# State-space layer: gate product on ScalarE and GpSimd, a new order of the last tiles, other buffers for the next stage's inputs

## The chip, the cores and the metric

The kernel runs on one core of a Trainium2 chip. The core has a matrix engine (TensorE, PE in the profile, with PEld for its weight loads), a vector engine (VectorE, DVE), an engine for functions of one operand (ScalarE, ACT), a general engine (GpSimd, POOL) and a queue that issues the DMAs (SyncE, SP). The metric is the device time of one execution in microseconds, the median over runs; less is better.

## The reference

Two layers of a causal decoder trunk, for a sequence of 1024 tokens of width 1024, in float32:

```python
for i in range(DEPTH):                      # DEPTH = 2
    h = rms_norm(x, pre_norm)
    h = dilated_attention_mixer(h, ...) if i % 2 == 0 else s5_mixer(h, ...)
    x = x + rms_norm(h, post_norm)

def s5_mixer(h, ...):
    proj = h @ w_in                         # 1024 x 2048
    u, z = proj[..., :SSM_WIDTH], proj[..., SSM_WIDTH:]
    y = s5_scan(u, ...)                     # 64 groups of 16 channels, 64 complex states each
    g = gelu(y)
    y = g * sigmoid(g @ w_glu + b_glu)      # the GLU
    return (y * silu(z)) @ w_out
```

The change lies in the second layer, `s5_mixer`: in the product z * sigmoid(z) of its gate, in the order of the last tiles of `h @ w_in`, and in the buffers through which g reaches the GLU's matmuls.

## The kernel before, in words

**Precision by halves.** Every operand of a large matmul is held as two parts, a rounded high part and a low part that is the rest (`split`, L79 to L87: ACT makes the high part, DVE subtracts for the low part). A product is the sum of three matmuls: high by high, high by low, low by high (`proj_part`, L102). A weight tile of 128 output columns is loaded and split by `load_w` (L90); raw, high and low tiles have two buffers each, so a weight tile takes the buffers of the one two before it.

**Tiles and halves.** The tokens are two halves (th = 0, 1) of 512. A tile of a projection is one weight tile times one half: 8 blocks of depth by 3 matmuls, 24 matmuls into one bank of matmul memory (PSUM). `in_order` (L759) runs over the weight tiles and calls `use(e, th, ps)` on each result, and then `after(t)` with the running number t of the tile.

**The state-space layer** (`layer1`, L1402) has 16 weight tiles: e = 0 to 7 give u, e = 8 to 15 give z. With `start="half"` the first two weight tiles are run by token halves, all others tile by tile, both halves of one before the next. `use_u` copies u out to memory. `use_z` makes the gate, in two instructions: ACT takes tanh(z/2) into a slot, and DVE forms (tanh + 1) * z, with z read from the bank; the result is written to memory (`z_dr`).

Between the tiles runs the scan, for eight groups of channels, each in stages that `run(t)` starts at a fixed tile: loads, `ssm_input`, `ssm_taps`, `ssm_states` and `ssm_outputs`. `ssm_states` (L1347) is a chain through the engines: PE pv (L1359), three DVE products (L1360 to L1362), a GpSimd sum (L1363), four DVE scans (L1366), a GpSimd product (L1368), DVE products and X (L1370 to L1372). `ssm_outputs` (L1376) multiplies X and the taps on PE (py, L1386 and L1387), and forms the GELU: ACT (L1388, L1389), two GpSimd instructions (L1390, L1391), ACT (L1392), DVE (L1393); the result goes to memory (`y_dr`, L1394). The last group's outputs come after tile 29 of 0 to 31.

**The GLU** (`glu`, L1445) reads y back in another order (`y_view`): 16 loads of 128 x 512, 8 groups for each token half, each followed by a split into the tiles g0 and g1. Its first two weight tiles are run as a block (`start="block"`): four banks are filled over the first 7 of 8 depth blocks, in the order (0,0), (1,0), (0,1), (1,1) of weight tile and half, and then the last depth block of all four. The later weight tiles run one by one.

**Buffers.** Short-lived tiles of 128 x 512 come from a ring, `c.slot` (L50), which takes turns between two tags with 3 and 4 buffers. The pool pb has six large tiles, b0 to b5: b1 holds the taps of groups 0 to 3, b3 those of groups 4 to 7; b4 and b5 hold the high and low part of the layer's normed input for the first token half, b0 and b2 for the second. The GLU's inputs take b1 (high) and b3 (low) for the first half, b4 and b5 for the second; its weights for the output projection later take b1 and b4. The tag O (4 buffers of 128 x 1024) holds the outputs of attention, and later the two post-norm weights; in the state-space layer it is otherwise unused.

**Order of the work.** Each engine, and the SP queue, works in the order of its own list. The lists are written by a planner which simulates the program with estimated times and lets the instruction of the highest rank go that is ready by them; the rank is the place in the program, and `high_priority(AHEAD)` moves a block 600 places forward. So a change of one instruction's engine or place can shift others in all lists. An instruction that waits holds up everything behind it on its engine.

Of the kernel before, what the change touches and what calls it, by code (L numbers as in the profile page):

```python
# [15 lines left out]
F32 = mybir.dt.float32  # L16
F32R = mybir.dt.float32r
I32 = mybir.dt.int32
AF = mybir.ActivationFunctionType
ALU = mybir.AluOpType  # L20
# [3 lines left out]
P = 128  # L24
S = 1024
D = 1024
KT = 8
H = 512
# [85 lines left out]
def proj_half(c, w, h):  # L114

    pool, tag = ((c.psj, "psj"), (c.pst, "pst"))[c.banks % 2]
    c.banks += c.wide
    ps = pool.tile([P, H], F32, tag=tag, name="psj")
    proj_part(c, ps, w, h, range(KT))
    return ps  # L120
# [638 lines left out]
def in_order(c, srcs, h, use, after=None, start=None, ws=()):  # L759

    t = 0

    def one(e, th, ps):
        nonlocal t
        use(e, th, ps)
        if after:
            after(t)
        t += 1  # L770

    ws = list(ws) or [load_w(c, srcs[e]) for e in range(2 if start else 0)]
    if start == "block":
        jobs = [(e, th) + ((c.psj, "psj"), (c.psl, "psl"))[th] for th in range(2) for e in range(2)]
        pss = [pool.tile([P, H], F32, tag=tag, name="psb") for _, _, pool, tag in jobs]
        for ks in (range(KT - 1), (KT - 1,)):
            for ps, (e, th, _, _) in zip(pss, jobs):
                proj_part(c, ps, ws[e], h[th], ks)
                if ks[0]:
                    one(e, th, ps)  # L780
    elif start == "half":
        for e in range(2):
            one(e, 0, proj_half(c, ws[e], h[0]))
        pss = [c.psj.tile([P, H], F32, tag="psj", name="psj") for _ in range(2)]
        for part in range(2):
            cs = slice(part * 256, part * 256 + 256)
            for e in range(2):
                proj_part(c, pss[e][:, cs], ws[e], [x[:, :, cs] for x in h[1]], range(KT), part == 0)
                if part:
                    one(e, 1, pss[e])  # L790
    c.wide = 1 if start == "half" else c.wide
    for e in range(len(ws), len(srcs)):
        w = load_w(c, srcs[e])
        for th in range(2):
            one(e, th, proj_half(c, w, h[th]))
    c.banks = c.wide = 0

# [599 lines left out]
def y_view(c, et, th):  # L1397

    return bass.AP(c.y_dr.tensor, c.y_dr.offset + et * P * S + th * 4 * 16384, [[P, P], [16384, 4], [1, P]])


def layer1(c, a, h1, ws):  # L1402

    nc, tc = c.nc, c.tc
    c.ssm = c.es_pa.enter_context(tc.tile_pool(name="ssm", bufs=1, side="left", reuse_waits="tile"))
    def use_u(et, th, ps):
        ut = c.slot("ut")
        with tc.high_priority(AHEAD):
            nc.scalar.copy(ut.rearrange("p (i n) -> p i n", i=4)[:, ::-1, :], ps.rearrange("p (i n) -> p i n", i=4))
            dst = bass.AP(c.u_dr.tensor, c.u_dr.offset + et * P * S + (1 - th) * 4 * 16384, [[P, P], [16384, 4], [1, P]])  # L1410
            nc.sync.dma_start(dst, ut.rearrange("p (i n) -> p i n", i=4))

    def use_z(et, th, ps):
        z = c.slot("z1")
        with tc.high_priority(AHEAD):
            nc.scalar.activation(z, ps, AF.Tanh, scale=0.5)
            nc.vector.scalar_tensor_tensor(z, z, 1.0, ps, op0=ALU.add, op1=ALU.mult)
            nc.sync.dma_start(c.z_dr[et, :, th * H:th * H + H], z)

    groups = [Ssm(c, a, e) for e in range(8)]  # L1420
    c.taps = []
    at = [[] for _ in range(40)]
    for e in range(8):
        t = (11 * e + 2) // 4
        for stage, d in ((ssm_loads, (-1, 2)[e] if e < 2 else 3), (ssm_input, 5), (ssm_taps, 6), (ssm_states, 7), (ssm_outputs, 10)):
            at[t + d + 1].append((stage, e))

    def run(t):
        for stage, e in at[t + 1]:
            if stage is ssm_loads and e == 1:  # L1430
                with tc.issue_after(groups[0].load_U.ins):
                    stage(groups[e])
            else:
                stage(groups[e])

    def use(e, th, ps):
        (use_u if e < 8 else use_z)(e % 8, th, ps)

    run(-1)
    in_order(c, [a["ssm_w_in"][e] for e in range(16)], h1, use, run, start="half", ws=ws)  # L1440
    for t in range(32, 39):
        run(t)


def glu(c, a):  # L1445
    nc, tc = c.nc, c.tc
# [1 line left out]
    nc.sync.dma_start(bh, a["b_glu"])  # L1448
    nc.vector.tensor_scalar(bh, bh, 0.5, None, op0=ALU.mult)
    g, y2 = [], []  # L1450
    for th, tags in enumerate((("b1", "b3"), ("b4", "b5"))):
        g.append([c.pb.tile([P, KT, H], F32R, tag=t, name=f"g{th}{t}") for t in tags])
        for et in range(8):
            y = c.slot("gy")
            nc.sync.dma_start(y.rearrange("p (i n) -> p i n", i=4), y_view(c, et, th))
            split(c, g[th][0][:, et, :], g[th][1][:, et, :], y)
    y2.append([c.pb.tile([P, KT, H], F32R, tag=t, name=f"y0{t}") for t in ("b0", "b2")])
# [185 lines left out]
```

## Time and profile before

| what | value |
|---|---|
| median of 3 runs | 1691.89 us (1691.3 to 1694.68) |
| the profiled execution, its own time | 1692.35 us |
| its span on the core | 1690.6 us |
| mean granted clock of TensorE | 0.991 |
| PE, DVE, ACT, POOL busy | 98%, 60%, 42%, 27% of the span |
| z tiles in the state-space layer | 1375.6 to 1497.5 us |
| loads of gy, first and last issue | 1489.7, 1512.3 us |

Times in the text are microseconds from the start of the span, of that one execution. A row of a list of stretches gives its bounds and length, and then how long each engine was busy in it. A row of the chain of waits gives a start, a length, and the engine and line or the transfer that the end of the program hung on. "PE busy" counts a matmul until its modelled end, and the matmuls overlap: the pace is read from the starts or from how many ran in a stretch.

### The profile page before, as it was taken

How to read it: one execution, taken by the hardware profiler on the slowest of the kernel's cores; microseconds unless marked ns; L12 is line 12 of the kernel's file. 1: busy time of each engine (PE TensorE's matmuls, PEld its weight loads, DVE VectorE, ACT ScalarE, POOL GpSimd, SP SyncE). 2: the span in 40 equal slices, each digit the busy share in tenths (PEclk: the TensorE clock that was granted, in tenths of full speed). 3: DMA queues.
4: the chain of work that ended last, by engine and by line, in shares of the span. 5: the costliest groups of instructions: out<-in, count | busy, mean ns of one | idle time of the engine just before them, and what ended most of it. 6: DMA issues, size and time to landing. Idle time of an engine off the chain costs nothing.

```text
span 1690.6 us, 26330 instructions
## 1 busy us (share of the span) xinstructions
PE 1655.9 (98%) x9714; PEld 1395.1 (83%) x9714; DVE 1012.3 (60%) x2511; ACT 712.8 (42%) x1730; POOL 452.8 (27%) x301
## 2 busy tenths in 40 slices
PE   8999999999999999999999999998999999999998
PEld 6889999978888888888888888886888887867886
DVE  8698898625454554545455454567462788845533
ACT  5232232226456464646556464654352222243411
POOL 2000000132241514324252523303220344513121
PEclk9999999999999999999999999998999999989999
DMA  6222455531232423233142323228146978365432
GB/s 238 83 55 101 148 176 163 166 105 54 89 104 65 118 69 98 83 93 92 58 136 71 110 83 101 87 69 225 63 155 195 262 223 250 112 206 164 147 119 87
DMA packets 176857, 212.19 MB, mean 126 GB/s; under 512 B 37443, under 2 KB 133462, under 8 KB 176728
## 3 DMA queue, kind: packets, MB, share of 16 engines
q1 hardware_dynamic: 176728, 210.52, 41.7%
q8 instruction: 76, 1.25, 0.3%
q14 instruction: 53, 0.43, 0.1%
HBM read 153.51 MB, written 56.96 MB: 124 GB/s over the span
## 4 chain that ended last, share of the span: by engine, by line
PE 85%; DVE 7%; DMA 4%; issue 1%; POOL 1%; ACT 1%; SPq 0%; DVEq 0%; POOLq 0%; ACTq 0%
PE psj L110 45%; PE psq L373 10%; PE psl L471 5%; PE pso L548 4%; PE pt L499 4%; PE pso L865 3%; PE pso L866 3%; PE pso L867 3%; PE psb L110 1%; PE pso L574 1%; DVE T L1366 1%; DMA fz<-on_dr 1%; PE psv L234 1%; PE psv L233 1%; PE psv L232 1%
## 5 line engine op out<-in xcount | busy, mean ns | idle before, releaser
L110 PE MATMUL psj<-hh,whi 128*128 128x512 f32 x896 | 358.1, 400 | 0.0
L110 PE MATMUL psj<-hh,wlo 128*128 128x512 f32 x896 | 358.1, 400 | 0.0
L110 PE MATMUL psj<-hl,whi 128*128 128x512 f32 x896 | 355.2, 396 | 0.0
L84 POOL TENSOR_TENSOR wlo<-wraw,whi 128x1024 fp32r<-128x1024 f32 x48 | 115.2, 2400 | 394.8 <-ACT whi L83 379.7
L110 PEld LDWEIGHTS psj<-hh,whi 128*128 128x128 f32 x896 | 168.8, 188 | 37.0
L110 PEld LDWEIGHTS psj<-hh,wlo 128*128 128x128 f32 x896 | 168.8, 188 | 36.4
L110 PEld LDWEIGHTS psj<-hl,whi 128*128 128x128 f32 x896 | 168.7, 188 | 36.3
L488 ACT ACTIVATE lg<-lg,nm 128x128 f32<-128x128 f32 (+1 forms) x384 | 168.2, 442 | 37.0 <-DVE nm L483 37.0
L477 DVE CUSTOM_DVE_ANT_0 lg<-psl,T 128x128 f32<-128x128 f32 (+1 forms) x384 | 110.6, 347 | 89.1 <-PE psl L471 89.1
L83 ACT CAST whi<-wraw 128x1024 fp32r<-128x1024 f32 x80 | 83.7, 1046 | 161.9 <-PE psj L110 108.0
L373 PE MATMUL psq<-whi,v 128*128 128x256 f32 x640 | 120.3, 284 | 0.0
L110 PE MATMUL psj<-h1h,whi 128*128 128x512 f32 (+1 forms) x272 | 104.9, 386 | 1.1 <-ACT h1h L83 1.1
L84 DVE TENSOR_TENSOR ph<-pt,ph 128x512 fp32r<-128x512 f32 (+2 forms) x160 | 96.7, 622 | 15.3 <-ACT ph L83 13.1
L84 DVE TENSOR_TENSOR kl<-psj,kh 128x512 fp32r<-128x512 f32 x48 | 33.2, 691 | 119.3 <-ACT kh L83 118.8
L110 PE MATMUL psj<-h1l,whi 128*128 128x512 f32 (+1 forms) x272 | 104.2, 383 | 0.2 <-DVE h1l L84 0.2
L110 PE MATMUL psj<-h1h,wlo 128*128 128x512 f32 (+1 forms) x272 | 104.0, 383 | 0.0
L83 ACT CAST ph<-pt 128x512 fp32r<-128x512 f32 (+2 forms) x160 | 81.5, 529 | 46.5 <-PE pt L499 45.5
L373 PEld LDWEIGHTS psq<-whi,v 128*128 128x128 f32 x640 | 100.0, 189 | 1.2 <-issue 1.2
L373 PE MATMUL psq<-wlo,v 128*128 128x256 f32 x320 | 91.2, 285 | 0.7 <-DVE wlo L84 0.7
L548 PE MATMUL pso<-ph,vs 128*128 128x256 f32 (+1 forms) x544 | 86.6, 284 | 0.0
L499 PE MATMUL pt<-identr,lg 128*128 128x128 f32 x560 | 82.2, 276 | 0.0
L1232 POOL TENSOR_TENSOR Ks<-Ks,O 128x16 f32<-128x16 f32 x8 | 4.3, 536 | 284.5 <-ACT Ks L1230 284.5
(284 smaller groups left out, 3691.0 us busy)
## 6 DMA issues: line engine op xcount, KB each, us to landing
wraw<-in_w_in_dram SPq DMA_DIRECT2D x56, 512.0 KB
mw<-wt_dr SPq DMA_DIRECT2D x48, 256.0 KB
v<-in_w_v_dram SPq DMA_DIRECT2D x20, 512.0 KB
vp<-v_dr SPq DMA_DIRECT2D x16, 512.0 KB
wraw<-in_ssm_w_in_dram SPq DMA_DIRECT2D x16, 512.0 KB
v_dr<-v SPq DMA_DIRECT2D x30, 256.0 KB
rot_dr<-rt SPq DMA_DIRECT2D x48, 128.0 KB
ca_dr<-ca SPq DMA_DIRECT2D x32, 144.0 KB
```

The source lines that it names most:

```text
L83: nc.scalar.copy(hi, src)
L84: return (engine or nc.vector).tensor_tensor(lo, src, f32(hi), op=ALU.subtract)
L110: nc.tensor.matmul(ps, a[:, s], b[:, k, :], start=first and k == 0 and n == 0, stop=k == KT - 1 and n == 2, skip_group_check=True)
L373: nc.tensor.matmul(o, r[x][:, k, ts], w[y][:, k, :], skip_group_check=True, start=i in (0, 4, 5) and t % 2 == k == n == 0, stop=k == 3 and ...
L471: nc.tensor.matmul(psl[:, h, o], x[HEADS[h], qs], y[HEADS[h], ks], start=j == js[0] and n == 0, stop=n == 2, skip_group_check=True)
L477: nc.vector.tensor_tensor_reduce(lg[:, h, j, 0:w], psl[:, h, o], bt[:, h, 256 - w:256], scale=1.0, scalar=-3.0e38, op0=ALU.add, op1=ALU.ma ...
L488: nc.scalar.activation(lg[:, h, j, 0:w], lg[:, h, j, 0:w], AF.Exp, bias=nm[:, h, b:b + 1], accum_out=ms[:, col:col + 1])
L499: c.nc.tensor.transpose(pt[:, n * P:(n + 1) * P], lg[:, h, j, part * P:part * P + P], c.ident)
L548: nc.tensor.matmul(o, l, r, start=n == 0, stop=n == len(jobs) - 1, skip_group_check=True)
L865: nc.tensor.matmul(ps, gh[:, k, ts], wh[:, k, :], start=k == 0, stop=False)
L866: nc.tensor.matmul(ps, gh[:, k, ts], wl[:, k, :], start=False, stop=False)
L867: nc.tensor.matmul(ps, gl[:, k, ts], wh[:, k, :], start=False, stop=k == KT - 1)
```

## The change

Three edits in one:

- `use_z` takes two slots instead of one. ACT writes tanh(z/2) into the first and copies z from the bank into the second; GpSimd adds 1 to the first and multiplies the second by it. The two GpSimd instructions and the write to memory stand outside the high-priority block.
- In `in_order` with `start="half"`, the last two weight tiles are loaded together and run by token halves: (14,0), (15,0), (14,1), (15,1) instead of (14,0), (14,1), (15,0), (15,1). For the other callers `pairs` is 0 and nothing changes.
- In `glu`, y is loaded into a ring of six halves of three O tiles instead of slots, and the tiles of the GLU's inputs change: b1 and b4 for the first token half, b5 and b3 for the second.

```diff
@@ in_order
-    c.wide = 1 if start == "half" else c.wide
-    for e in range(len(ws), len(srcs)):
+    c.wide = int(start == "half")
+    pairs = 2 if start == "half" else 0
+    for e in range(len(ws), len(srcs) - pairs):
         w = load_w(c, srcs[e])
         for th in range(2):
+            one(e, th, proj_half(c, w, h[th]))
+
+    ws = [(e, load_w(c, srcs[e])) for e in range(len(srcs) - pairs, len(srcs))]
+    for th in range(2):
+        for e, w in ws:
             one(e, th, proj_half(c, w, h[th]))
     c.banks = c.wide = 0
@@ layer1
     def use_z(et, th, ps):
-        z = c.slot("z1")
+        t, z = c.slot("zt"), c.slot("z1")
         with tc.high_priority(AHEAD):
-            nc.scalar.activation(z, ps, AF.Tanh, scale=0.5)
-            nc.vector.scalar_tensor_tensor(z, z, 1.0, ps, op0=ALU.add, op1=ALU.mult)
-            nc.sync.dma_start(c.z_dr[et, :, th * H:th * H + H], z)
+            nc.scalar.activation(t, ps, AF.Tanh, scale=0.5)
+            nc.scalar.copy(z, ps)
+        nc.gpsimd.tensor_scalar(t, t, 1.0, None, op0=ALU.add)
+        nc.gpsimd.tensor_tensor(z, z, t, op=ALU.mult)
+        nc.sync.dma_start(c.z_dr[et, :, th * H:th * H + H], z)
@@ glu
-    for th, tags in enumerate((("b1", "b3"), ("b4", "b5"))):
+    ring = [x[:, n * H:n * H + H] for x in (c.outs.tile([P, D], F32, tag="O", name="gy", bufs=4) for _ in range(3)) for n in range(2)]
+    for th, tags in enumerate((("b1", "b4"), ("b5", "b3"))):
         g.append([c.pb.tile([P, KT, H], F32R, tag=t, name=f"g{th}{t}") for t in tags])
         for et in range(8):
-            y = c.slot("gy")
+            y = ring[(8 * th + et) % 6]
             nc.sync.dma_start(y.rearrange("p (i n) -> p i n", i=4), y_view(c, et, th))
             split(c, g[th][0][:, et, :], g[th][1][:, et, :], y)
```

## The prediction

> **What bounds the kernel now.** I read the stretches between the state-space layer and the output tiles first, engine by engine:
>
> ```profile
> 1477.40:1493.80 16.40, 15.25 (x81) 12.50 (x80) 7.49 (x10) 6.98 (x12) 5.12 (x5) 1.00 0.58 191
> 1493.80:1502.45 8.65, 5.17 (x10) 2.41 (x11) 6.65 (x9) 5.73 (x9) 0.00 (x0) 0.67 0.85 244
> 1502.45:1506.30 3.85, 3.85 (x11) 2.98 (x10) 1.39 (x2) 0.87 (x3) 0.00 (x0) 0.50 1.09 348
> 1506.30:1525.00 18.70, 18.55 (x78) 14.59 (x76) 8.60 (x11) 7.74 (x13) 2.91 (x3) 0.98 0.54 156
> 1525.00:1527.10 2.10, 1.20 (x5) 0.68 (x5) 2.08 (x2) 2.10 (x3) 1.31 (x2) 1.00 0.72 223
> 1527.10:1682.00 154.90, 154.90 (x667) 125.48 (x668) 67.10 (x134) 40.59 (x76) 36.19 (x27) 1.00 0.41 131
> ```
>
> Columns: stretch, length, busy time of PE, weight load, DVE, ACT, POOL, then granted clock, DMA share and rate. After 1527.10 PE is never idle at clock 1.00, so no edit there can save anything (the tags of the GLU inputs also free two buffers for the last weights earlier; that is worth nothing under this cover). The loss is at 1493.80 to 1527.10, where the state-space layer hands over to the GLU: PE is busy 5.17 of 8.65 us, and then runs 3.85 us at clock 0.50.
>
> The end of the chain of waits says on what it hangs:
>
> ```profile
> 1480.00 2.05 DMA y_dr<-Y
> 1486.11 1.77 POOL Y L1391
> 1490.13 3.85 DMA gy<-y_dr
> 1496.33 4.41 DMA gy<-y_dr
> 1501.43 22.48 PE psb L110 x84
> 1525.02 2.03 DVE wlo L84
> 1527.10 49.93 PE psj L110 x212
> 1577.49 16.86 PE psj L110 x72
> ```
>
> Undisturbed, 72 matmuls take 16.86 us, 0.2342 us each. The GLU's first block holds 4 tiles of 24, so 96, and 4 more matmuls of the next weight tile ran before 1527.10. That is 100 x 0.2342 = 23.42 us of work in 33.30 us: **9.88 us are lost here**. The cause in the chain is the load of gy, the layer's outputs read back from memory. The DMA queue in order of time:
>
> ```profile
> 1486.74 2.87 SPq L1394 DMA_DIRECT2D y_dr<-Y  x2
> 1489.67 1.59 SPq L1455 DMA_DIRECT2D gy<-y_dr  x3
> 1491.30 0.50 SPq L1418 DMA_DIRECT2D z_dr<-z  x1
> 1494.52 3.64 SPq L1455 DMA_DIRECT2D gy<-y_dr  x6
> ```
>
> No gy leaves before 1489.67, after the last group's write, although by the chain the seventh of eight groups was written from 1480.00. The loads use slots of the two-tag ring that the z tiles hold too, and the low halves of the first GLU half go into b3, which holds the taps of groups 4 to 7.
>
> Two smaller waits lie inside the layer:
>
> ```profile
> PE py L1387 <- DVE X L1372: 2.1, 1, 2.1
> ...
> PE py L1387 <- POOL Y L1391: 1.1, 1, 1.1
> ```
>
> ```profile
> 1414.90:1418.40 3.50, 3.47 (x16) 3.48 (x17) 2.90 (x4) 0.08 (x1) 0.05 (x1) 0.51 0.94 321
> ```
>
> The 2.1 us wait is followed by 3.50 us at clock 0.51, which did 16 matmuls; half of the stretch, about 1.7 us, is lost to the clock. So the layer loses 2.1 + 1.7 + 1.1 = 4.9 us.
>
> The Trainium skill (TensorE: Matmul & The Clock Gate, Part 1: The HAM clock gate) says that the clock falls to half after an idle window of about 3.4 us. The half agrees with 0.50 and 0.51, the length does not: one 2.1 us wait was enough here. By the page's rule a leftover wait of 2 us would cost 2 us; by the trace it costs nearly 4, and I go by the trace.
>
> **The inputs' ring and the tags.** Nothing is added: still 16 loads, 16 casts and 16 subtractions. Three O tiles give six halves, and nobody else writes them after the attention output stage. So the first six loads wait only for their group's outputs, and can leave before 1480. The low halves now go into b4, the high half of the layer's first normed input, which is free when the tiles of the first token half are done; by the new tile order that is two tiles before the layer's end, 2 x 24 x 0.2342 = 11.2 us ahead of 1493.8, instead of one tile. What is late next: group 6 and 7's loads, then the eight of the other half, which need the ring halves back. In the queue above, three loads took 1.59 us and six took 3.64 us to issue, and the chain gives 3.85 and 4.41 us for a load with its wait; ten loads from about 1482 are in by about 1500, and the second token half starts 21 matmuls x 2 tiles = 9.8 us after 1493.8, at 1503.6. So the waits on gy should go, and the slow clock with them. Bounds: the whole 9.88 us, or nothing if the loads do not move.
>
> I leave 1.0 us in the block, for one late operand; the wait for the next GLU weights stays, since their buffer is freed only in the block's last matmuls. Before, 1525.00 to 1527.10 was 2.10 us for 4 matmuls' 0.94, 1.2 us lost; I take 1.3. Saved: 9.88 - 1.0 - 1.3 = **7.6 us**.
>
> **The last tiles by token halves.** The same 96 matmuls, reordered. Weights 15 are now needed one tile earlier, and their buffer is that of weights 13:
>
> ```profile
> 1462.60 1.05 ACT L83 CAST whi<-wraw 128x1024 fp32r<-128x1024 f32 x1 [6.57 <-PE psj L110]
> ...
> 1479.28 1.03 ACT L83 CAST whi<-wraw 128x1024 fp32r<-128x1024 f32 x1
> ```
>
> ```profile
> 1471.79 1.19 DVE L84 TENSOR_TENSOR wlo<-wraw,whi 128x1024 fp32r<-128x1024 f32 x1
> ```
>
> ```profile
> 1465.98 0.39 PE L1387 MATMUL py<-X,CA 128*128 128x128 f32 x2
> ```
>
> Tile (14, first half) starts when group 6's py matmuls end at about 1466.2 and takes 24 x 0.2342 = 5.6 us, to 1471.8. The third matmul of (15, first half) wants the low part at about 1472.3; where DVE has it now it ends at 1472.98. I take 0.7 us, between 0 (DVE reaches it earlier, having lost two z products before it) and 2.5 (a wait of 1.2 and the clock). The weight buffer of the GLU's tile 0 is freed one tile later too, at about 1488 where its cast now runs at 1479.28. Cast and subtraction take 1.03 + 1.19 = 2.2 us, done by 1491, before 1493.8: nothing, with 2.8 us of cover.
>
> **The gate halves.** The DVE product leaves, an ACT copy and two GpSimd instructions come, 16 times, from 1375 to 1494. The groups of that time (line, busy, mean ns, idle):
>
> ```profile
> L1391 POOL TENSOR_TENSOR Y<-Y,Y 128x512 f32<-128x512 f32 x12 | 17.5, 1460 | 0.8
> ...
> L1371 DVE TENSOR_TENSOR T<-Sg,T 64x512 f32<-64x512 f32 x10 | 13.8, 1377 | 0.2
> ...
> L1417 DVE SCALAR_TENSOR_TENSOR z<-z,psj 128x512 f32<-128x512 f32 x16 | 10.8, 677 | 0.7 <-ACT z L1416 0.7
> ...
> L1416 ACT ACTIVATE z<-psj 128x512 f32<-128x512 f32 x16 | 9.3, 591 | 21.1 <-PE psj L110 21.1
> ...
> L1390 POOL TENSOR_SCALAR Y<-Y 128x512 f32<-128x512 f32 x12 | 8.6, 720 | 12.9 <-ACT Y L1389 12.2
> ...
> L1361 DVE TENSOR_TENSOR T<-Sg,pv 64x512 f32<-64x512 f32 x9 | 6.2, 690 | 0.1
> ```
>
> ```profile
> 1375.00:1493.80 118.80, 115.54 (x619) 98.27 (x617) 96.61 (x131) 36.05 (x59) 56.59 (x54) 0.99 0.62 185
> ```
>
> ACT: 16 x 0.591 = 9.5 us more on 36.05 of 118.80, hidden under its idle time; a matmul bank is then free after ACT alone and no longer waits for DVE. POOL: 16 x (0.720 + 1.460) = 34.9 us more on 56.59, so 91.5 of 118.8. These are in order with the scan's own steps (L1363, L1368) and the GELU's (L1390, L1391): a pair ahead of one of them makes it 2.2 us late, then DVE's X and PE's py behind it. The z writes on the SP queue now wait for POOL as well, and the loads behind them wait with them. DVE: 16 x 0.677 = 10.8 us less. But L1371 takes 1377 ns where L1361, of the same shape, takes 690: the one that reads two operands from SBUF is stretched by 0.69 us on average beside POOL's work. If each pair stretches one such instruction, 16 x 0.69 = 11.0 us come back, and DVE stays at 96.8.
>
> The Trainium skill (SBUF — State Buffer, Who interferes with whom) speaks against this edit: a DVE instruction with two SBUF inputs and a GpSimd instruction that reads SBUF lock each other out entirely. The product taken away read one operand from PSUM and, by that rule, locked nothing. If every GpSimd pair kept DVE waiting for its whole length, DVE would come to 96.6 - 10.8 + 34.9 = 120.7 us, more than the stage.
>
> So the layer's price is 0 in my sum: X comes 0.7 us earlier without a product before it, or about as much later with a stretched instruction. Bounds: 4.9 us won (both waits gone) to 15.6 us lost (first rival).
>
> **Sum.** 7.6 - 0.7 - 0 = 6.9 us. The profiled execution took 1692.35 us (span 1690.6, 1.75 around it): 1685.4. It was 0.46 above the median of 1691.89, so the runs' median becomes **1685.0**.
>
> **Rivals.**
> First, slower: GpSimd becomes the link that sets py. If in each of the last four groups, whose chains run beside z tiles, one pair stands ahead of a chain step and py has no slack, PE waits 2.2 us and loses 1.7 us to the clock: 4 x 3.9 = 15.6, 1700.6. For it: two of these groups wait already, and 81% of DVE's stage is full. Against: the other groups do not wait, and POOL is idle for half of the stage. It undoes the gain from 1.7 us a group. Chance 0.15.
>
> Second, the wait changes its owner: weights of GLU tiles 0 and 1 come after 1493.8, each 2.2 us of cast and subtraction, and 4 us of slow clock cost 2: 6.4 of the 6.9 are gone, 1691.4. For it: the two reordered tiles hold both weight buffers longer. Against: the cover of 2.8 us. Chance 0.12.
>
> Third, the change does not do what it says: the planner leaves the loads behind the last group's writes, as at 1489.67, and the block loses its 9.88 us as before: about 1692. For it: nothing but the order of one queue decides. Chance 0.06.
>
> Fourth, more: the layer's own 4.9 us go too, since a z product stood on DVE before X: 1680.1. Against: POOL's added work. Chance 0.17.
>
> **How the numbers follow.** The forecast keeps 0.50. Differences under 0.2%, 3.4 us, can't be told from none here. Faster: forecast and fourth, 0.67. Same: second (but for its lower edge) and third, 0.17. Slower: the first, and 0.01 of the second: 0.16. The forecast's own range is 1682 to 1688.5. To hold 8 in 10 I go from 1680, the fourth's time, to 1692.5, the third's, and leave out most of the first.
>
> **What would show it.** Right: gy loads leave before 1480, psb follows psj with under 1 us of waits, the clock stays near 1.00 through the block, and from the block's first matmul to the tile after it pass about 25 us instead of 33. The gate: DVE's L1371 or X stretched, POOL near 90 us in the stage. Wrong: PE's waits on py grow or appear in more groups, with clock near 0.5 behind them; or psb waits on weights; or gy still leaves after the last y_dr.

## The result: slower

The changed kernel takes 1701.03 us (median of 4 runs, 1699.99 to 1702.91), the kernel before took 1692.29 us (4 runs, 1691.3 to 1694.68). The ratio on record is **1.0055, 95% interval 1.0041 to 1.0069**; it is not the plain quotient of the two medians, which is 1.0052. The forecast was 1685.0 us, range 1680.0 to 1692.5: wrong in sign. The profiled execution of the changed kernel took 1700.58 us, its span is 1698.8 us against 1690.6, so 8.2 us longer.

Line numbers grow by 6 in the changed kernel, and by 9 behind the gate: py is L1392/L1393, X is L1378, the GELU L1394 to L1399, y_dr L1400, gy L1464. The gate is L1422 and L1423 (ACT), L1424 and L1425 (GpSimd), L1426 (write). I cut both traces at the same work: the pv matmuls of groups 4, 5 and 7, the block's first matmul, and the tile behind the block. Before, in the columns of the list of stretches:

```profile
1393.80:1420.14 26.34, 24.23 (x124) 20.74 (x123) 19.69 (x27) 8.10 (x13) 11.01 (x11) 0.94 0.94 261
1420.14:1455.30 35.16, 35.16 (x186) 29.66 (x185) 29.97 (x44) 10.07 (x16) 19.17 (x18) 1.00 0.65 193
1455.30:1493.82 38.52, 37.35 (x201) 31.36 (x199) 29.00 (x39) 11.93 (x20) 15.66 (x15) 1.00 0.38 123
1493.82:1527.10 33.28, 28.77 (x101) 20.66 (x101) 18.70 (x24) 16.44 (x25) 4.22 (x4) 0.85 0.70 205
```

After, the same stretches, then the whole layer from 1375.00, the two stretches of slow clock around the ends of its longest waits, and the rest of the program up to where the forecast's last row ended:

```profile
1393.50:1426.10 32.60, 24.06 (x123) 20.57 (x122) 20.09 (x24) 10.95 (x20) 20.86 (x17) 0.90 0.84 232
1426.10:1462.00 35.90, 35.52 (x187) 29.83 (x186) 26.00 (x32) 10.85 (x20) 30.23 (x26) 1.00 0.71 222
1462.00:1510.63 48.63, 40.26 (x201) 33.15 (x199) 46.85 (x54) 18.68 (x34) 36.89 (x28) 0.93 0.36 114
1510.63:1535.30 24.67, 24.21 (x100) 18.59 (x100) 6.52 (x8) 8.20 (x14) 9.66 (x6) 1.00 0.54 169
...
1375.00:1510.60 135.60, 118.35 (x618) 99.81 (x616) 111.00 (x128) 47.95 (x85) 104.26 (x82) 0.95 0.58 178
1417.52:1424.36 6.84, 3.34 (x15) 3.34 (x16) 6.68 (x8) 2.44 (x5) 4.98 (x3) 0.50 0.72 228
1485.80:1492.63 6.83, 5.17 (x12) 4.11 (x13) 6.68 (x7) 0.63 (x1) 6.04 (x5) 0.50 0.39 115
...
1535.30:1690.20 154.90, 154.87 (x667) 125.47 (x668) 71.05 (x137) 42.26 (x79) 38.64 (x28) 1.00 0.43 136
```

The last row is as long as before (154.90 us, 667 matmuls, clock 1.00), so everything happens ahead of it. The block of the GLU went from 33.28 to 24.67 us at clock 1.00: **8.6 us won, where the forecast said 7.6**. But the block starts 16.8 us later (1510.63 against 1493.82). Group 4 is 6.3 us longer, groups 5 and 6 0.7, the last stretch of the layer 10.1, and the first mark lies 0.3 earlier; 16.8 - 8.6 = 8.2, the difference of the spans.

PE's waits in the changed kernel from 1260 on (engine, what it waited for, us in total, times, the longest):

```profile
PE py L1393 <- DVE X L1378: 11.4, 4, 8.5
PE psj L110 <- DVE wlo L84: 5.3, 1, 5.3
...
PE psb L110 <- ACT whi L83: 0.6, 1, 0.6
```

The waits of psb on gy are gone. In their place stand one wait of 8.5 us for X in group 4, one of 5.3 us for the low part of weights 15, and around the end of each a stretch of 6.8 us at clock 0.50. Part of it passes while PE still waits: PE works at half clock for 3.3 us behind the first wait, which ends at 1421.02, and for 5.2 us behind the second, which ends at 1487.46. About half of these times is lost, 1.7 and 2.4 us.

**How group 4 became late.** GpSimd's list of the changed kernel, in order of time, with idle time and its releaser in brackets:

```profile
1377.98 1.61 POOL L1424 TENSOR_SCALAR zt<-zt 128x512 f32<-128x512 f32 x1
1379.56 1.60 POOL L1374 TENSOR_TENSOR X<-Cg,T 128x508 f32<-128x508 f32 x1
...
1381.16 1.69 POOL L1425 TENSOR_TENSOR z<-z,zt 128x512 f32<-128x512 f32 x1
...
1387.45 3.29 POOL L1397 TENSOR_TENSOR Y<-Y,Y 128x512 f32<-128x512 f32 x2
```

The gate's pair stands ahead of the GELU product of group 2 (L1397), whose two instructions end at 1390.74; before, the later of them ended at 1389.26. The planner works with estimates of such times. In the list that it wrote, both writes of that group's outputs now stand behind a run of loads in the SP queue:

```profile
1394.07 1.73 SPq L1343 DMA_DIRECT2D taps<-k_dr  x4
...
1396.37 1.35 SPq L1400 DMA_DIRECT2D y_dr<-Y  x2
```

Before, they stood on either side of three loads of taps:

```profile
1390.76 0.37 SPq L1394 DMA_DIRECT2D y_dr<-Y  x1
1391.76 1.78 SPq L1337 DMA_DIRECT2D taps<-k_dr  x3
1394.54 0.34 SPq L1394 DMA_DIRECT2D y_dr<-Y  x1
```

The next group's GELU overwrites the tile that is being written out, so ACT is held at its first step. After:

```profile
1402.39 0.60 ACT L1394 ACTIVATE Y<-py 128x512 f32<-128x512 f32 x1 [10.03 <-DMA y_dr<-Y]
```

Before:

```profile
1396.18 0.60 ACT L1388 ACTIVATE Y<-py 128x512 f32<-128x512 f32 x1 [4.34 <-DMA y_dr<-Y]
```

ACT goes on 6.2 us later. The end of that GELU (L1399) stands in DVE's list ahead of group 4's scans, so DVE waits for it, then the scans and X come, and PE behind X:

```profile
1408.13 0.69 DVE L1399 SCALAR_TENSOR_TENSOR Y<-Y,Y 128x512 f32<-128x512 f32 x1 [9.38 <-ACT Y L1398]
1410.01 3.50 DVE L1372 TENSOR_TENSOR_SCAN T<-rho,T 128x128 f32<-128x128 f32 x4 [1.18 <-POOL T L1369]
...
1419.23 1.74 DVE L1378 TENSOR_TENSOR X<-X,T 128x508 f32<-128x508 f32 x1
```

**What the pairs themselves cost.** Groups of like instructions of the changed kernel, GpSimd and DVE, 1375 to 1511 (busy time, mean ns of one, idle time before them):

```profile
L1424 POOL TENSOR_SCALAR zt<-zt 128x512 f32<-128x512 f32 x14 | 25.2, 1800 | 3.8 <-ACT zt L1422 3.8
L1425 POOL TENSOR_TENSOR z<-z,zt 128x512 f32<-128x512 f32 x14 | 20.8, 1485 | 0.7
...
L1372 DVE TENSOR_TENSOR_SCAN T<-rho,T 128x128 f32<-128x128 f32 x40 | 25.4, 694 | 3.9 <-POOL T L1369 3.6
L1377 DVE TENSOR_TENSOR T<-Sg,T 64x512 f32<-64x512 f32 x10 | 13.7, 1370 | 0.2
L1378 DVE TENSOR_TENSOR X<-X,T 128x508 f32<-128x508 f32 x10 | 12.3, 1245 | 0.5
L1376 DVE TENSOR_TENSOR T<-Sg,T 64x512 f32<-64x512 f32 x10 | 10.7, 1071 | 0.3
```

The same DVE groups before, 1375 to 1494 (L1371, the counterpart of L1377, is in the prediction with 1377 ns):

```profile
L1366 DVE TENSOR_TENSOR_SCAN T<-rho,T 128x128 f32<-128x128 f32 x40 | 20.2, 568 | 0.3
...
L1372 DVE TENSOR_TENSOR X<-X,T 128x508 f32<-128x508 f32 x10 | 8.8, 919 | 0.1
L1370 DVE TENSOR_TENSOR T<-Sg,T 64x512 f32<-64x512 f32 x10 | 8.6, 857 | 0.3
```

One GpSimd pair takes 1.80 + 1.49 = 3.3 us and not 2.2, and the scans, X and L1376 are stretched by 5.2 + 3.5 + 2.1 = 10.8 us, about as much as the old product cost DVE.

### The profile page after: what moved, and what is told of

Read it like the earlier page. It is cut to its first block, busy times and chain, and to the rows that moved or that the text cites. A ratio compares the mean times of both kernels' runs of the same rounds, so it can differ in the third digit from the quotient of the medians.

```text
span 1698.8 us, 26348 instructions
## 1 busy us (share of the span) xinstructions
PE 1653.9 (97%) x9714; PEld 1394.2 (82%) x9714; DVE 1018.1 (60%) x2495; ACT 718.3 (42%) x1746; POOL 510.1 (30%) x333
## 5 line engine op out<-in xcount | busy, mean ns | idle before, releaser
L110 PEld LDWEIGHTS psj<-hl,whi 128*128 128x128 f32 x896 | 168.7, 188 | 36.3
```

The lines of the kernel that those rows point to most:

```text
L110: nc.tensor.matmul(ps, a[:, s], b[:, k, :], start=first and k == 0 and n == 0, stop=k == KT - 1 and n == 2, skip_group_check=True)
```

## The experiments

The three edits are called gate, tile order and buffers (ring and tags); a diff is against the changed kernel unless the text names another. Every ratio is to the kernel before on the same chip, with its 95% interval; that kernel's medians there were 1690.36 to 1691.45 us, so a ratio can't be had from the medians of this table (for the gate alone the medians differ by 10.3 us, where the ratio gives 11.7 and its interval 9.0 to 14.6). The stages are in us, by the starts of the first pv matmul of a group and of the first and last matmul of the block, read from the time line of PE.

| kernel | median | ratio | group 4 | 5, 6 | 7 to block | block |
|---|---|---|---|---|---|---|
| before | 1692.29 | 1 | 26.2 | 35.3 | 38.6 | 30.6 |
| after | 1701.03 | 1.0055 (1.0041-1.0069) | 32.6 | 35.9 | 48.7 | 22.7 |
| gate alone | 1701.72 | 1.0069 (1.0053-1.0086) | 31.7 | 35.7 | 48.5 | 25.0 |
| old gate | 1688.37 | 0.9986 (0.9973-1.0000) | 28.2 | 35.3 | 39.8 | 23.6 |
| no ring | 1703.38 | 1.0075 (1.0060-1.0090) | 32.3 | 35.3 | 49.6 | 25.4 |
| gate alone, product on DVE | 1687.39 | 0.9983 (0.9973-0.9993) | 24.0 | 35.3 | 41.2 | 22.9 |
| gate alone, GpSimd on 32 columns | 1687.26 | 0.9981 (0.9972-0.9991) | 25.7 | 35.3 | 39.6 | 22.9 |
| GELU in tag O, gate alone | 1694.65 | 1.0024 (1.0014-1.0033) | 25.0 | 35.9 | 48.6 | 23.8 |
| GELU in tag O, before | 1686.11 | 0.9977 (0.9966-0.9988) | 22.2 | 35.3 | 38.3 | 28.9 |
| buffers alone | 1687.19 | 0.9984 (0.9974-0.9993) | 28.0 | 35.3 | 41.0 | 22.3 |
| gate alone, two-operation addition | 1700.63 | 1.0051 (1.0034-1.0068) | 34.7 | 35.3 | 44.6 | 26.0 |
| after, two-operation addition | 1702.04 | 1.0068 (1.0049-1.0086) | 32.7 | 36.3 | 50.7 | 22.3 |
| that addition and GELU in tag O, gate alone | 1692.95 | 1.0010 (1.0001-1.0020) | 27.6 | 35.3 | 44.4 | 24.9 |

A wait for g0b just ahead of the block's first matmul counts in the column before it: 4.8 us in the gate alone, 3.9 without the ring, 2.4 with the product on DVE and with GpSimd on 32 columns; in the changed kernel a wait of 0.6 for weights stands there. The hand-over, this wait and the block together, took 30.6 us before, 29.8 in the gate alone, 29.4 without the ring and 23.3 in the changed kernel.

### Which of the three edits costs

Old gate, with the new tile order and the buffers:

```diff
-        t, z = c.slot("zt"), c.slot("z1")
+        z = c.slot("z1")
         with tc.high_priority(AHEAD):
-            nc.scalar.activation(t, ps, AF.Tanh, scale=0.5)
-            nc.scalar.copy(z, ps)
-        nc.gpsimd.tensor_scalar(t, t, 1.0, None, op0=ALU.add)
-        nc.gpsimd.tensor_tensor(z, z, t, op=ALU.mult)
-        nc.sync.dma_start(c.z_dr[et, :, th * H:th * H + H], z)
+            nc.scalar.activation(z, ps, AF.Tanh, scale=0.5)
+            nc.vector.scalar_tensor_tensor(z, z, 1.0, ps, op0=ALU.add, op1=ALU.mult)
+            nc.sync.dma_start(c.z_dr[et, :, th * H:th * H + H], z)
```

> The changed kernel with the old gate product (ACT tanh, DVE product); tile order and the ring of gy as changed. Theory G (the GpSimd pairs delay the scan's chain): the 8.5 us wait of py on X falls back to about 2 us and the 5.3 us wait on the low weights goes; 1684 to 1687 us, and ACT waits little for gy inside the layer. Theory L (casts of gy stand early in ACT's list and wait for loads that the SP queue issues behind the output writes): ACT still waits 7 to 10 us three times for gy, py still waits about as long, 1697 to 1701 us.

Measured: 1688.37 us, ratio 0.9986 (0.9973 to 1.0000), 1.4 us above the range of theory G. PE's wait for X is 3.8 us at the longest, the one for weights 15 is 1.1 us; ACT still waits 25.1 us for gy, so that part of theory L came true without its time.

The changed kernel without the ring, gy through slots as before, the new tags kept:

```diff
-            y = ring[(8 * th + et) % 6]
+            y = c.slot("gy")
```

> The changed kernel with gy in the slots as before; gate, tile order and tags as changed. Theory G: the layer's waits stay (X about 8 us, low weights about 5 us) and the block loses its 8 to 10 us again: 1703 to 1709 us. Theory L: no cast of gy before the last group's outputs, py waits at most 3 us in all; the block's loss is back: 1691 to 1695 us.

Measured: 1703.38 us, ratio 1.0075 (1.0060 to 1.0090). By these two ratios the ring is worth 0.20% or 3.4 us in the whole change, but their intervals overlap; the hand-over is 6.0 us shorter with it (29.4 to 23.3).

The gate alone, in the kernel before (old order, old tags, no ring):

```diff
-    pairs = 2 if start == "half" else 0
+    pairs = 0
...
-            y = ring[(8 * th + et) % 6]
+            y = c.slot("gy")
...
-    for th, tags in enumerate((("b1", "b4"), ("b5", "b3"))):
+    for th, tags in enumerate((("b1", "b3"), ("b4", "b5"))):
```

> Only the gate product moves to ACT and GpSimd; the rest is the kernel before. Theory G: waits of py grow by 8 to 15 us: 1700 to 1707 us. Theory L: within 3 us of before, 1690 to 1695 us, the block's loss at the hand-over as before.

Measured: 1701.72 us, ratio 1.0069 (1.0053 to 1.0086). The two halves of the change add up: 1.0069 x 0.9986 = 1.0055, the ratio of the whole. So **the gate costs 0.69% or 11.7 us, the rest gains 0.14% or 2.4 us**. The forecast had 0 and 6.9. The interval of that gain reaches 1.0000, so it may be nothing.

### Do the early loads of gy cost something?

The ring lets the loads of gy go as soon as their group is written, and the first leaves early indeed (SP queue of the changed kernel):

```profile
1344.63 0.37 SPq L1464 DMA_DIRECT2D gy<-y_dr  x1
```

Their casts then stand in ACT's list inside the layer, where ACT waits for them. Two kernels hold the loads until group 6 has been written, one as changed and one with the old gate:

```diff
+    c.last_store = groups[6].store.ins
...
+            with tc.issue_after(c.last_store):
-            nc.sync.dma_start(y.rearrange("p (i n) -> p i n", i=4), y_view(c, et, th))
+                nc.sync.dma_start(y.rearrange("p (i n) -> p i n", i=4), y_view(c, et, th))
```

> The changed kernel, with each load of gy ordered on the SP queue behind the output write of group 6, so that no cast of gy can be planned inside the scan. Theory L: the waits of ACT on gy inside the layer go, py waits at most 3 us, the hand-over stays short: 1684 to 1688 us. Theory G: the gate still delays the chain, the waits of py stay above 8 us: 1697 to 1702 us. Where both act, in between.

Measured, with the new gate: 1697.60 us, ratio 1.0044 (1.0028 to 1.0059), 0.11% under the changed kernel; the intervals overlap.

> The old gate product, the new tile order, and the ring of gy with the loads ordered behind group 6's output write. If early casts of gy cost the 3 to 4 us in the run without the gate edit: 1683 to 1686 us, py waits under 3 us, no wait of ACT on gy before the last group's chain. If they do not: 1687 to 1690 us.

Measured, with the old gate: 1690.22 us, ratio 0.9996 (0.9986 to 1.0005), 0.10% above the same without the hold, and those intervals overlap too. ACT's waits on gy fell from 25.1 us in 5 times to 7.6 us in 4, but the block now waits for its weights, whose cast stands behind the late casts of gy in ACT's list:

```profile
PE psb L110 <- ACT whi L83: 4.9, 1, 4.9
```

With the loads held, group 4 is back at 26.3 us (28.2 with early loads, 26.2 before), but the last stretch of the layer is 43.4 us long instead of 39.8. So the early loads are at most a small part of the loss, and holding them moves the wait.

### ACT's copies, or GpSimd?

The gate alone again, with ACT's tanh and copy in two slots, but the product on DVE from the copy:

```diff
-        nc.gpsimd.tensor_scalar(t, t, 1.0, None, op0=ALU.add)
-        nc.gpsimd.tensor_tensor(z, z, t, op=ALU.mult)
-        nc.sync.dma_start(c.z_dr[et, :, th * H:th * H + H], z)
+            nc.vector.scalar_tensor_tensor(z, t, 1.0, z, op0=ALU.add, op1=ALU.mult)
+            nc.sync.dma_start(c.z_dr[et, :, th * H:th * H + H], z)
```

> Only the gate edit, but with the product on DVE: ACT takes tanh and copies z as in the changed kernel, and one DVE instruction multiplies from the copy; GpSimd does nothing for it. If GpSimd's 32 instructions are the cause of the gate's 10 us: within 3 us of before, 1689 to 1695 us, the wait of py on X for group 4 back to 2 to 3 us. If the ACT copies and the second slot are the cause: 1698 to 1702 us.

Measured: 1687.39 us, ratio 0.9983 (0.9973 to 0.9993), 1.6 us under the range expected for this. ACT's copies and the second slot cost nothing; taking GpSimd out takes the whole loss out. Does its time cost, or the additional link through one more engine? With the links kept and the work cut to 32 of 512 columns, so that 15 of 16 of the product are left out:

```diff
-        nc.gpsimd.tensor_scalar(t, t, 1.0, None, op0=ALU.add)
-        nc.gpsimd.tensor_tensor(z, z, t, op=ALU.mult)
+        nc.gpsimd.tensor_scalar(t[:, 0:32], t[:, 0:32], 1.0, None, op0=ALU.add)
+        nc.gpsimd.tensor_tensor(z[:, 0:32], z[:, 0:32], t[:, 0:32], op=ALU.mult)
```

> Only the gate edit, but the two GpSimd instructions of each z tile work on 32 of the 512 columns (15 of 16 of the product are left out). The links stay: ACT, GpSimd, GpSimd, write. Theory (it is the time that GpSimd spends, and what the planner makes of that time): near the kernel before or under it, 1686 to 1692, the writes of y_dr stand among the loads of taps again, GpSimd's busy time in the layer falls from about 100 us to about 65. Rival (an additional link through GpSimd is enough, however short): 1697 to 1702, as the gate edit alone.

Measured: 1687.26 us, ratio 0.9981 (0.9972 to 0.9991). The two groups in that kernel, and ACT's wait for the writes:

```profile
L1424 POOL TENSOR_SCALAR zt<-zt 128x32 f32<-128x32 f32 x16 | 10.0, 624 | 14.0 <-ACT zt L1422 9.0 <-DMA gy<-y_dr 5.0
...
L1425 POOL TENSOR_TENSOR z<-z,zt 128x32 f32<-128x32 f32 x16 | 8.0, 501 | 1.5 <-POOL zt L1424 0.5
```

```profile
ACT Y L1394 <- DMA y_dr<-Y: 5.7, 2, 4.6
```

The link is harmless; **the work that GpSimd does is the cause**, by its own time and by what the planner makes of it: with the short instructions the writes of y_dr stand between the taps again, and ACT is held 4.6 us at most instead of 10.

Neither of these two kernels has the ring, and yet the hand-over takes 25.2 us in both, against 30.6 before. So the buffers are not the only thing that shortens it; what does it here was not tried.

The whole change with the product on DVE, by the edit shown above:

> The whole change, but the product (tanh + 1) * z is formed on the vector engine from the copy that ACT made; GpSimd gets none of the 32 instructions. Theory (the GpSimd instructions of the gate are the whole cause of the loss, the rest of the change pays as forecast): the 14.3 us between the gate edit alone (1701.7) and the same with the product on the vector engine (1687.4) come off the changed kernel's 1701.0 too, less what the early gy casts on ACT cost: 1685 to 1690, and PE's wait for X in group 4 falls from 8.5 us to about 2. Rival (the loads and casts of gy, moved into the layer, are enough to hold group 4 by themselves): 1695 or more, with ACT held 8 to 10 us on y_dr as in the changed kernel.

Measured: 1689.49 us, ratio 0.9991 (0.9981 to 1.0000), within the expected range. Of the 0.0055 that the change lost, 0.0064 come back. PE's waits there:

```profile
PE psj L110 <- DVE wlo L84: 3.9, 1, 3.9
PE py L1393 <- DVE X L1378: 3.2, 1, 3.2
```

The wait in group 4 fell from 8.5 to 3.2 us, not to the 2 that I expected, and the one for weights 15 stays at 3.9 (1.1 with the old gate), so that one is not GpSimd's alone.

### How much goes by way of ACT's wait?

The hold on ACT comes from the two buffers of the GELU tile Y1. Four of the otherwise unused tag O take it away, in the gate alone and in the kernel before:

```diff
-        T1, T2 = (c.ssm.tile([P, 4, P], F32, name=n, tag=n, bufs=2) for n in ("Y1", "Y2"))
+        T1 = c.outs.tile([P, D], F32, tag="O", name="Y1", bufs=4)[:, 0:H].rearrange("p (g n) -> p g n", g=4)
+        T2 = c.ssm.tile([P, 4, P], F32, name="Y2", tag="Y2", bufs=2)
```

> Only the gate edit as changed, and the first GELU tile of each group in buffers of the idle tag O, so that ACT need not wait until the output write of the group before has landed. If the gate costs by way of that write (later on the SP queue, ACT held 10.7 us, then GELU, scan, X and py late): the 10.7 us wait goes, py of group 4 waits under 3 us, 1691 to 1696 us. If it costs by the GpSimd steps themselves, the wait of py stays above 5 us: 1698 to 1702 us.

Measured, gate alone: 1694.65 us, ratio 1.0024 (1.0014 to 1.0033).

> The kernel before, with the same other buffers for the GELU tile: the measure for the run with the gate edit. ACT waits 4 us there and py 2.1 us before; if that wait hangs on the write too, 3 to 4 us faster, 1687 to 1689 us; if it hangs on the rest of the chain, no change, 1690 to 1693 us.

Measured, kernel before: 1686.11 us, ratio 0.9977 (0.9966 to 0.9988), 0.9 us faster than expected. So this buffer is worth 0.23% without the gate and 0.45% with it. The gate's price is 1.0069 with the hold and 1.0024 / 0.9977 = 1.0047 without: **about 3.7 of the 11.7 us go by way of the late writes, 8 remain**. By the widths of the three intervals these 3.7 us are uncertain by about as much again (an estimate). The stages agree with them: the gate makes group 4 longer by 5.5 us with the hold and by 2.8 without. The 8 us lie in group 4 (25.0 against 22.2 us) and above all in the last stretch (48.6 against 38.3), of which the block gives 5.1 back. There PE waits in that kernel (gate alone, GELU in tag O):

```profile
PE psb L110 <- ACT g0b L83: 4.7, 1, 4.7
PE py L1394 <- POOL Y L1398: 4.4, 1, 4.4
```

The first stands just ahead of the block. The second is a late group's matmuls waiting for the GELU product on GpSimd itself, which shares its list with the pairs.

### Why a pair takes 3.3 us, and whether that matters

GpSimd's additions of one shape have two prices in the trace of before. The group of the rotations, which the forecast had passed by:

```profile
L1285 POOL TENSOR_SCALAR rt<-rt 128x512 f32<-128x512 f32 x8 | 11.9, 1492 | 0.0
```

L1285 does one operation (times -1), as the gate's addition does; L1390, by which I had priced it, does two (times, plus) and averaged 720 ns. The fastest L1424 takes 1486 ns, the fastest of the GELU's form 617. The gate alone and the whole change, with the addition as "times 1, plus 1":

```diff
-        nc.gpsimd.tensor_scalar(t, t, 1.0, None, op0=ALU.add)
+        nc.gpsimd.tensor_scalar(t, t, 1.0, 1.0, op0=ALU.mult, op1=ALU.add)
```

> The gate alone on ACT and GpSimd as in the change, but GpSimd's addition written with two operations (times 1, plus 1) instead of one, the same result. In the traces the single form L1424 takes 1486 ns at the least, as L1285, the only other of that form, takes 1480 to 1507; the double form of the GELU, L1396, takes 617 at the least on the same shape. Theory (the form sets most of the addition's price, and GpSimd's time sets the loss): the instruction falls to 0.62 to 0.95 us, a pair to about 2.2 us, GpSimd's work to 35 us instead of 53; a third of GpSimd's added time goes, and the writes of y_dr stand among the taps again as with the short instructions, so 1690 to 1695. Rival (it is stretched by its neighbours on the vector engine, not by its form): the instruction stays at 1.5 to 2 us and the time at 1699 to 1703.

Measured: 1700.63 us, ratio 1.0051 (1.0034 to 1.0068); the intervals of this and of the gate alone overlap. The groups in that kernel, and PE's longest wait:

```profile
L1425 POOL TENSOR_TENSOR z<-z,zt 128x512 f32<-128x512 f32 x16 | 25.9, 1616 | 1.2
...
L1424 POOL TENSOR_SCALAR zt<-zt 128x512 f32<-128x512 f32 x16 | 16.1, 1006 | 5.0 <-ACT zt L1422 5.0
```

```profile
PE py L1393 <- DVE X L1378: 10.5, 1, 10.5
```

> The whole change with that same two-operation addition. Theory (form): the gate's remaining price as in the kernel with the gate alone, less the 2.4 us that tile order and buffers bring: 1688 to 1693, PE's wait for X in group 4 from 8.5 to 2 to 5 us. Rival (neighbours): 1698 to 1702, wait 8 us or more.

Measured: 1702.04 us, ratio 1.0068 (1.0049 to 1.0086). Half of the theory holds: **the form sets the price of the instruction** (1800 to 1006 ns, a pair from 3.3 to 2.6 us). The other half falls: the loss doesn't shrink with it. In the gate alone the last stretch became 3.9 us shorter (48.5 to 44.6), but group 4 became 3.0 us longer. There the two writes of group 2 stand among the taps again and still go late (SP queue of the gate alone with this addition):

```profile
1390.94 5.30 SPq L1343 DMA_DIRECT2D taps<-k_dr  x3
1396.35 0.37 SPq L1400 DMA_DIRECT2D y_dr<-Y  x1
...
1399.49 0.38 SPq L1400 DMA_DIRECT2D y_dr<-Y  x1
```

ACT is held on the second of them until 1404.43, and X is done at 1422.7, where the gate alone had it at 1418.8. Of the 5.3 us that three loads of taps take in the queue there, it waits 3.8 for a load of U (the waits of SP, 1390.9 to 1396.3):

```profile
SPq L1343 <- DMA U<-u_dr: 3.8, 1, 3.8
```

That wait is 1.6 us in the gate alone; what ties the taps to this load, and why it grew, the trace doesn't say. DVE's four groups shown above take 61.2 us in this kernel, 61.9 in the gate alone and 51.4 before, so shorter pairs stretch DVE hardly less; how much of the loss goes by that was not separated. With ACT's hold taken away as well (Y1 in tag O, gate alone):

> The gate alone with the two-operation addition, and the first GELU tile in buffers of tag O, so that ACT isn't held by the writes of y_dr. Theory (late writes carry the loss of group 4 in both forms; what remains, 8 us, is GpSimd's own time ahead of the last groups and shrinks with the pair, from 3.3 to 2.6 us): ratio to the kernel before 1.0000 to 1.0015, 1690.5 to 1693.5 us, group 4 at 22 to 25 us. Rival (what remains doesn't depend on the pair's length but on the links and stretched instructions of the vector engine): 1.0020 to 1.0030, 1694 to 1696 us, as with the one-operation form.

Measured: 1692.95 us, ratio 1.0010 (1.0001 to 1.0020), where the one-operation form gave 1.0024 (1.0014 to 1.0033), and 0.9977 is the base of both. The time is in the expected range of the theory; group 4 isn't (27.6 us, expected 22 to 25). So the remaining price went from 0.47% to 0.33%, 7.9 to 5.6 us, where the pairs went from 53 to 42 us: it goes down with their length, as far as intervals that overlap can say. The last stretch is 4.2 us shorter for it.

### Buffers alone, and a candidate

Buffers without the new tile order and with the old gate:

```diff
-    pairs = 2 if start == "half" else 0
+    pairs = 0
```

> Only the buffers (ring of O halves and the new tags) with the old gate and the old tile order. Theory (the 7.6 us of the hand-over are there, but gy casts stand early in ACT's list and cost some us in the layer; the tile order costs the 0.7 us of the forecast): 1687 to 1689, block of psb 23 to 25 us. First rival (the tile order cost several us in the kernel with both): 1684 to 1686, the whole 7.6 us. Second rival (the low halves get b4 too late without the new order): 1690 to 1692, block 28 us or more.

Measured: 1687.19 us, ratio 0.9984 (0.9974 to 0.9993). The block has no loss left in it, 97 matmuls in 22.49 us at clock 1.00, and the layer pays for it (the stretch of the block, then ACT's wait for gy from 1370 to 1500, both of this kernel):

```profile
1497.29:1519.78 22.49, 22.49 (x97) 17.89 (x95) 8.70 (x13) 8.83 (x14) 2.96 (x2) 1.00 0.58 180
```

```profile
ACT g0b L83 <- DMA gy<-y_dr: 28.9, 6, 8.5
```

The same kernel with the new tile order is the one called old gate, 0.9986: the order changes nothing that can be told. Block and layer here are -8.4 and, in group 4 and from 7 on, +1.8 and +2.4 us against before; the second rival of this expectation (28 us or more in the block) is out.

Old gate, new order and tags, no ring, and Y1 in tag O (the edits shown above together):

> Candidate: old gate, new tile order and tags, no ring (gy through slots, so no early casts), and the first GELU tile in buffers of tag O, so that ACT does not wait for the writes of y_dr. Theory (both gains add: 4.6 us by the GELU buffers, and part of the hand-over by tile order and tags): 1682 to 1685. Rival (without the ring the loads of gy leave as late as before, so tile order and tags bring nothing): 1685.5 to 1688.

Measured: 1686.89 us, ratio 0.9976 (0.9967 to 0.9986), as Y1 in tag O alone (0.9977). Without the ring, order and tags bring nothing: from its first matmul to its last the block takes 29.2 us, where the buffers alone gave 22.3.

So three ways that leave GpSimd out of the gate beat the kernel before, and with it the changed one, by an interval that excludes 1: Y1 in tag O (with or without the order), the buffers alone, and the gate's product on DVE from ACT's copy. Their intervals overlap, so they aren't told apart.

## Why the prediction was wrong

**The hand-over: right, and in size partly luck.** 9.88 us were said to be lost in 33.30; the changed kernel takes 24.67 from the block's first matmul to the same place, so 8.6 us are won where 7.6 were forecast. But not all of it is the buffers': with the new gate and order, the ring makes the hand-over 6.0 us shorter, and two kernels without a ring have 5.4 us less than before. The signs named for it came: gy leaves before 1480, psb waits 0.6 us, the clock stays at 1.00.

**But "nothing is added" by the buffers: wrong.** The 16 casts are the same, yet they moved: the first load left at 1344.63 and not at 1489.67, and the casts went into ACT's list inside the layer, where they hold ACT for 25 us (with the old gate) to 29 us (buffers alone). With the buffers alone the layer is about 4 us longer (+1.8 and +2.4), so they are worth 2.7 us in the end (ratio 0.9984) and not 7.6. That the early loads cause it is shown for group 4, which is back at 26.3 us when they are held, and not for the last stretch. The prediction asked what is late next among the loads, and never what stands behind the casts.

**The last tiles by token halves: the price was mis-sized in its place and right in sum.** 0.7 us was forecast for weights 15, bounds 0 to 2.5. Measured is a wait of 5.3 us, plus 2.4 us of half clock (12 matmuls take 5.24 us from 1487.46, where they need 2.81). The low part is formed at 1486.21, behind the scans of group 7 in DVE's list, not ahead of them (time line of DVE, changed kernel):

```profile
1483.65 2.63 DVE L1372 TENSOR_TENSOR_SCAN T<-rho,T 128x128 f32<-128x128 f32 x4
1486.21 1.20 DVE L84 TENSOR_TENSOR wlo<-wraw,whi 128x1024 fp32r<-128x1024 f32 x1
```

I had taken the time from where DVE had this instruction before, as if the lists would stay. With the old gate the wait is 1.1 us, and the order as a whole costs nothing that can be told (0.9986 against 0.9984). The cover of 2.8 us for the GLU's first weights fell short by 0.6 us (psb's wait on ACT whi).

**The gate halves: "the layer's price is 0" is the step that failed.** It measured 11.7 us (gate alone, by its ratio). Its parts, in order:
- ACT's 9.5 us are hidden, as forecast: with the product on DVE the gate isn't slower than before.
- GpSimd was to take 34.9 us more. One pair takes 3.3 us instead of 2.2, so 16 take 53. I priced the addition by L1390, 720 ns, the same shape in another form; the row of its own form, L1285 with 1492 ns, was in the profile. Of the 1.08 us that each was dearer, 0.8 are the form (1800 to 1006 ns by the two-operation run). This is a mis-sized term, and not the cause of the sign: with it mended the change stays slower. In the stage POOL went from 56.59 of 118.80 to 104.26 of 135.60 us, where I expected 91.5.
- DVE was to get 11.0 us back as stretched instructions, on L1371. The size was right (10.8) and the rows were others: L1377, the counterpart of L1371, stayed at 1370 ns (it was no limit: with the two-operation addition it takes 1666), and the scans, X and L1376 were stretched, which lie on the chain to py.
- "X comes 0.7 us earlier without a product before it, or about as much later" priced one DVE instruction. What set X was two steps further up: a GELU that ended later on GpSimd, a write that the planner then put behind loads, ACT held 10 us, DVE's list held behind it. The text listed the GELU's steps as in order with the pairs, and that writes on SP wait for POOL, but then gave the place a price of zero within bounds of 15.6, on the ground that POOL is idle for half of the stage.

The first rival had the sign, the engine and nearly the time (1700.6), with a chance of 0.15. Its mechanism was not met as put: not four waits of 2.2 us, but one of 8.5 in group 4, one of 5.3 for weights 15 and a few of 1 to 1.4 us. The ground against it, that POOL is idle half of the time, is what misled: idle time of an in-order engine is no cover when the engine idles because it waits for the same chain.

**DVE against GpSimd.** The Trainium skill (SBUF — State Buffer, Who interferes with whom) spoke against this edit: a DVE instruction with two SBUF inputs and a GpSimd instruction that reads SBUF lock each other out. The direction was right. Its extreme, DVE kept waiting for the whole of every pair (120.7 us in the stage), isn't what happened: DVE has 111.0 us in a stage that is 16.8 us longer, and part of the waiting may lie on GpSimd: the gate's two-operation addition averaged 1006 ns, where the GELU's of the same shape takes 617 at the least. Which of the two held the other in a given place was not tried.

**What stays open.** Why the wait for weights 15 is still 3.9 us with the product on DVE: the subtraction stands behind group 7's scans there as with the old gate, but it ends 21.2 us after that group's first pv instead of 18.3. Of the 10.1 us of the last stretch, 5.3 + 2.4 + 1.4 (the waits of py for X in group 6, 2.5, less the wait of 1.1 that was there before) + 0.6 (psb on ACT whi) are named; about 0.4 are not. What shortens the hand-over in the kernels without a ring. And why the wait for U ahead of the late write grew from 1.6 to 3.8 us in the kernel with the two-operation addition.

## What to carry to other kernels

Price work that is moved to an in-order engine by rows of the same form (operations as well as shape), and ask which steps of the critical chain stand behind it in that engine's list; the share of idle time says nothing about that. Where a planner writes the lists, a later result also moves writes and loads in other queues: follow each buffer that is written out to the instruction that waits to reuse it. A load that can leave earlier puts its consumer earlier into another engine's list, and what a repaired hand-over wins (8.4 us in the block with the buffers alone) can be paid back there in part (4.2 us in the layer).

## What the runs showed of the hardware that was not expected

- One GpSimd instruction has two prices for one shape: 128 x 512 with one operation takes 1480 ns at the least (L1285, 8 times, up to 1507; L1424 from 1486), with two operations 617 ns (L1390, L1396). Adding a second operation that changes nothing (times 1) made it 0.8 us shorter on average.
- On 32 of 512 columns the one-operation addition averaged 624 ns and the product 501, where the fastest took 287 and 253: even such short instructions lasted about twice their best on average. What stretched them was not tried.
- The slow clock has its own time. Around the waits of 8.5 and 5.3 us it was at 0.50 for 6.84 and 6.83 us, about twice the 3.41 us (1414.89 to 1418.30) at the 2.1 us wait of the prediction. It fell 2.1 us after PE had stopped in the kernel before, and in the changed one 3.6 us after the stop for weights 15 (1482.2 to 1485.8) and 5.0 us after the stop for X (1412.5 to 1417.5). So the longer wait did not cost more of PE's work at half clock: 3.3 us behind 8.5, 5.2 us behind 5.3. The waits of 1.0 and 1.4 us in group 6 left the clock at 1.00.
